# RWKV mixer: the key projection as three reduced matmuls on split operands in place of one fp32 matmul, and two buffers for gates and decays

## The chip, the cores and the metric

The kernel runs on one core of one Trainium2 chip. The metric is device microseconds of one execution; lower is better. Before the change three runs took 1544.76 to 1545.33 us, median 1544.91 us.

## The reference, cut to what matters

The program is one inference step of a two-layer decoder. Layer 0 mixes tokens with Mamba-2, layer 1 with RWKV-7; both are wrapped in SwiGLU blocks and end in a gated embedding. A prompt of 256 tokens and 8 samples of 4 tokens go through together as 288 columns, in float32. The part that the change touches is this:

```python
xx = u_prev - u
mixed = u[None] + xx[None] * mu[:, None, None, :]
xr, xw, xk, xv, xa, xg = mixed[0], mixed[1], mixed[2], mixed[3], mixed[4], mixed[5]
r = xr @ w_r
k = xk @ w_k
v = xv @ w_v
...
g = jax.nn.sigmoid(xg @ g1) @ g2
kk = heads(k * k_k)
decay = jnp.exp(-jnp.exp(heads(w)))
```

The weights r_wr, r_wk, r_wv are 1024 x 1024. The columns of k of one pair of heads feed the recurrence of that pair alone.

## The kernel before, in words

Activations lie features by tokens: 8 tiles of 128 features x 288 tokens. A product of weights and activations is made in one of two ways. `mm3` takes a weight tile that was split into a high part (`whi`, ScalarE, line 55) and a low part (`wlo`, VectorE, line 56), four tiles to a split, and an activation that was split likewise by `hilo` (lines 155 and 156), and issues three matmuls in the reduced type float32r (lines 147 to 149). A whole product takes the raw float32 weight from a second stream (`next_whole`) and the raw activation, and is one matmul instruction in float32, which the trace shows as two records. The split stream `ws` holds 224 tiles of the RWKV stage, the whole stream `wn` 88: 8 for `r_wa1`, 16 for `r_g1`, and 64 for `r_wk`. `ws.next` splits 16 tiles ahead of use.

The RWKV stage (lines 1046 and following) starts with `lead`, which makes `u` and `xx`, the token-shift difference, and the inputs of the decay and rate branches. Then, for each pair of heads p = 0 to 7, four generators are stepped in turn: `bulk` (decay, rate, and the projections k and r of pair p + 1), `bulk2` (gate and projection v of pair p), `prep` (the triangular solve's operands of pair p, with `scan`, `AA`, `BK`), and `chain` (the recurrence of pair p - 1, over four chunks, with small matmuls of 64 x 64). At p = 0, `mix` (line 1105) makes the mixed activations once for all pairs: for r and v it writes into a temporary `t` with two buffers that `hilo` then splits, for k it writes a float32 tile that is used as it is. `gates` (p = 0 alone) makes eight tiles `mg` and multiplies each by two whole tiles of `r_g1` (line 1082).

The framework's scheduler sets the order of each engine's instructions from these generators, so an edit at one place moves instructions everywhere in the stage. Each engine runs its own list in order. Three PSUM banks, 0, 1 and 7, serve the big products of the loop in turn.

The names in what follows: `lnb` holds constants of the sigmoid and comes from the constants that GpSimd makes out of a loaded table `r_const`; `sw` and `sa` are the decay's and rate's sigmoids; `rs_y` is the running sum of `sw` (line 1229); `E1` its exponential; `SVm`, `SAV` and `S` belong to `chain`.

Of the kernel before, what the change touches and what calls it, by code (L numbers as in the profile page):

```python
# [6 lines left out]
F32 = mybir.dt.float32  # L7
F32R = mybir.dt.float32r
# [8 lines left out]
KD = 8  # L17
KF = 22
# [969 lines left out]
def s84(ap):  # L988
    return ap.rearrange("p (b t) -> p b t", b=8)


class Rwkv:
# [81 lines left out]
    def gates(self):  # L1074

        nc, k = self.nc, self.k
        pg = [k.bank(n)[:, :NT] for n in "YR"]
        for kt in range(KD):
            m = [None] * kt + [self.t("mg", bufs=2)]
            self.mix(5, kt, m)  # L1080
            for i in range(2):
                nc.tensor.matmul(pg[i], k.wn.next_whole("r_g1", kt, i), m[kt], start=kt == 0, stop=kt == KD - 1)  # L1082
            yield
        t, u = k.tmp("s"), k.tmp("u")
        self.sigmoid(t, pg[0], 0.0)
        self.sigmoid(u[0:32], pg[1][0:32], 0.0)
        k.hilo(self.lgh, self.lgl, t)
        self.stack(self.lg2, u, slice(0, 32), slice(32, 64))
        yield
# [11 lines left out]
    def mix(self, i, kt, out):  # L1101

        k = self.k
        m = k.tmp("t") if out[kt] is None else out[kt]
        self.nc.vector.scalar_tensor_tensor(m, self.xx[kt], k.g(f"mu{i}")[:, kt:kt + 1], self.u[kt], ALU.mult, ALU.add)
        if out[kt] is None:
            if i == 0:
                out[kt] = k.A[8 + kt], k.A[16 + kt]
            else:
                if kt == 0:  # L1110
                    k.renew(24, 32)
                k.renew(32 + kt, 33 + kt)
                out[kt] = k.A[24 + kt], k.A[32 + kt]
            k.hilo(*out[kt], m)
# [9 lines left out]
    def proj(self, n, i, x, p):  # L1124

        k, d = self.k, self.d[p]
        ps = k.bank("main")[:, :NT]
        for kt in range(KD):
            if p == 0:
                self.mix(i, kt, x)  # L1130
            if n == "k":
                self.nc.tensor.matmul(ps, k.wn.next_whole("r_wk", kt, p), x[kt], start=kt == 0, stop=kt == KD - 1)  # L1132
            else:
                k.mm3(ps, k.ws.next("r_w" + n, kt, p), x[kt], kt == 0, kt == KD - 1)
            if kt < KD - 1:
                yield
        d[n] = self.t(n, bufs=2)
        k.act(d[n], ps, AF.Copy)
        yield

    def bulk(self, p):

        nc, k = self.nc, self.k
        col = slice(p, p + 1)
        if p == 0:
            k.renew(0, 8, F32)
            k.renew(8, 16)
            self.xk = k.A[0:8]
            self.xv, self.xr = [[None] * KD for _ in range(2)]
        d = self.d[p] = {}  # L1150
        for n, x, b in (("sw", self.lw, "w0"), ("sa", self.la, "a0")):
            ps = k.bank("main")[:, :NT]
            self.stacked(ps, k.ws.next("r_" + n[1] + "2", 0, p), x)
            d[n] = self.t(n)
            self.sigmoid(d[n], ps, k.g(b)[:, col])
        yield
        yield from self.proj("k", 2, self.xk, p)
        yield from self.proj("r", 0, self.xr, p)

    def bulk2(self, p):  # L1160

        nc, k = self.nc, self.k
        d = self.d[p]
        ps = k.bank("main")[:, :NT]
        k.mm3(ps, k.ws.next("r_g2a", 0, p), (self.lgh, self.lgl), True, False)
        self.stacked(ps, k.ws.next("r_g2b", 0, p), self.lg2, False)
        d["g"] = self.t("g", bufs=3)
        k.act(d["g"], ps, AF.Copy)
        yield
        yield from self.proj("v", 3, self.xv, p)  # L1170
        V, v = self.V, d["v"]
        SAV = d["SAV"] = self.t("SAV", [P, 2, 5, 64], bufs=2)
        k.act(s84(V)[:, :, 0:4], s84(v[:, 256:288]), AF.Copy)
        pv = k.bank("A")
        for ch in range(5):
            for h in range(2):
                rows = slice(64 * h, 64 * h + 64)
                nc.tensor.matmul(pv[rows, 64 * ch:64 * ch + 64], v[rows, 64 * ch:64 * ch + 64] if ch < 4 else V[rows],
                                 self.I[rows], start=True, stop=True)
        for h in range(2):  # L1180
            rows = slice(64 * h, 64 * h + 64)
            k.act(SAV[rows, h], pv[rows, :320].rearrange("p (c t) -> p c t", c=5), AF.Copy)
        yield
# [29 lines left out]
    def prep(self, p):  # L1213

        nc, k = self.nc, self.k
        d = self.d[p]
# [10 lines left out]

        c = k.tmp("rs_y")
        nc.vector.tensor_tensor_scan(c, self.scan, d["sw"], 0.0, ALU.mult, ALU.add)
        E1 = d["E1"] = self.t("E1", bufs=3)  # L1230
        E2, Ex = k.tmp("ss"), k.tmp("t")
        k.act(E1, c, AF.Exp, scale=-KAPPA)
        k.act(E2, c, AF.Exp, scale=KAPPA)
# [13 lines left out]
        nc.vector.scalar_tensor_tensor(rk, d["r"], k.g("r_k")[:, col], k2, ALU.mult, ALU.mult)  # L1247
        self.pad_mul(AR[:, :, 1], d["r"], E1, AR[:, 4, 0])
        nc.vector.tensor_tensor(kk, kk, y, ALU.mult)
# [15 lines left out]
        ps = [k.bank("A"), k.bank("A")]  # L1265
# [7 lines left out]
        ps = [k.bank("A"), k.bank("A")]  # L1273
# [17 lines left out]
        def chunks(i):  # L1291

            return 5 if i < 2 else 4
# [16 lines left out]
        def at(t):  # L1310
            return lambda ch: t[:, ch]
# [4 lines left out]
        ps = mms(at(XT), eye)  # L1316
        k.act(X, ps, AF.Copy)
        yield
        for i in range(1, 6):
            n = chunks(i)  # L1320
# [21 lines left out]
        ps = mms(full, eye)  # L1342
# [5 lines left out]
        ps = k.bank("A")[:, :320].rearrange("p (c t) -> p c t", c=5)  # L1348
# [7 lines left out]
        ps = mms(at(R), full)  # L1356
# [5 lines left out]
    def chain(self, p):  # L1362
# [3 lines left out]
        col = slice(p, p + 1)  # L1366
        AR, AA, BKt, SAV, TT, E1, S0 = self.AR[p % 2], d["AA"], d["BKt"], d["SAV"], d["TT"], d["E1"], d["S0"]
        H = [(h, slice(64 * h, 64 * h + 64), slice(64 - 64 * h, 128 - 64 * h)) for h in range(2)]
# [37 lines left out]
        def solved(ch):  # L1406
# [5 lines left out]
            if ch < 4 and S is not None:  # L1412
                st["Se"] = self.t("Se", [P, 64])
                k.act(st["Se"], S, AF.Copy, scale=E1[:, 64 * ch + 63:64 * ch + 64])

        def state(ch):

            ps, S = k.bank("R"), st["S"]
            e = E1[:, 64 * ch + 63:64 * ch + 64]
            for h, rows, _ in H:  # L1420
# [21 lines left out]
        def samples():  # L1442
# [8 lines left out]
            nc.vector.tensor_tensor(S0, S0, ps.rearrange("p (b i) -> p b i", b=8), ALU.add)  # L1451
            nc.vector.tensor_tensor(S0, S0, s84(E1[:, 256:288])[:, :, 3:4].to_broadcast([P, 8, 64]), ALU.mult)
            nc.sync.dma_start(k.io["wkv_s"][p], S0)
# [165 lines left out]
    return np.ascontiguousarray(v.reshape(-1, P).T)  # L1619


COUNT = {"ffn": 24 * KF, "ple": 80, "mamba": 520, "rwkv": 224}
WHOLE = {"rwkv": 88}


def weight_tiles(x, stages):
# [97 lines left out]
def launch(x, stages, run):  # L1724
# [5 lines left out]
          for n, a in ins.items()}  # L1730
    units = [-(-max(1, sum(c.get(s, 0) for s, _, _ in stages)) // UT) for c in (COUNT, WHOLE)]
    for n, u in zip(("w", "wn"), units):
# [21 lines left out]
```

## Time and profile before

| | |
|---|---|
| profiled execution | 1545.45 us, its span 1543.6 us |
| three runs | median 1544.91 us (1544.76 to 1545.33) |
| PE busy | 1524.0 us, 99% of the span |
| VectorE busy | 1099.9 us, 71% |
| ScalarE busy | 972.9 us, 63% |
| RWKV stage | from about 976 to about 1290 us of the span |

A matmul's record is longer than the time from its start to the next matmul's, since matmuls are pipelined; the chain of work that ended last cuts the records to what each adds, and its steps are used for PE here. The same holds to a lesser degree on VectorE and ScalarE, where the distance between starts is used.

### The profile page before, as it was taken

To read this page: it belongs to the slowest core of one execution; us is meant where nothing else is said; L and a number is where in the kernel's file an instruction comes from. 1 tells how busy PE (TensorE), PEld (TensorE's weight loads), DVE (VectorE), ACT (ScalarE), POOL (GpSimd) and SP (SyncE) were. 2 spreads that over 40 slices of the span, in tenths; PEclk is the share of its full clock that TensorE was granted. 3 is DMA by queue.
4 is the path that set the end of the run, shared out by engine and by line. 5 is a ranking of instruction groups with operands and counts; after the bars stand their busy time and mean duration, and the time that the engine had idled before them with its cause. 6 is when DMAs were issued, how large, how long until landed. Compare 5 with 4: busy or idle time off the path is not lost.

```text
span 1543.6 us, 35587 instructions
## 1 busy us (share of the span) xinstructions
PE 1524.0 (99%) x14178; PEld 1422.4 (92%) x14178; DVE 1099.9 (71%) x2321; ACT 972.9 (63%) x2217; POOL 46.0 (3%) x143
## 2 busy tenths in 40 slices
PE   9999999999999999999999999999999999999997
PEld 8999998989989999999999999777777778999997
DVE  7666578888888766656876655887766778666566
ACT  7555458989887655554755554766666746555545
POOL 0000003112100000000000000100000000000000
PEclk9999999999999999999999999999999999999999
DMA  7555563765665555555555555531222224555551
GB/s 245 168 169 166 164 213 116 248 221 198 228 223 197 171 166 165 166 168 171 161 170 168 168 164 164 178 109 59 78 84 65 63 72 153 170 168 165 164 168 57
DMA packets 75574, 243.48 MB, mean 158 GB/s; under 512 B 11728, under 2 KB 16976, under 8 KB 75408
## 3 DMA queue, kind: packets, MB, share of 16 engines
q1 hardware_dynamic: 75408, 241.21, 48.6%
q8 instruction: 111, 1.82, 0.5%
q14 instruction: 55, 0.45, 0.1%
HBM read 226.54 MB, written 14.64 MB: 156 GB/s over the span
## 4 chain that ended last, share of the span: by engine, by line
PE 93%; DVE 4%; DMA 1%; ACT 1%; issue 1%; SPq 0%; POOL 0%; DVEq 0%; POOLq 0%; ACTq 0%
PE bank L147 26%; PE bank L149 26%; PE bank L148 25%; PE bank L1307 2%; PE bank L1132 1%; PE bank L770 1%; PE bank L1449 1%; PE bank L1421 1%; PE bank L774 1%; PE bank L766 1%; PE bank L641 1%; PE bank L1187 1%; DVE wlo L56 1%; PE bank L1381 1%; PE bank L1082 0%
## 5 line engine op out<-in xcount | busy, mean ns | idle before, releaser
L147 PE MATMUL bank<-act,whi 128*128 128x288 f32 x2760 | 825.0, 300 | 6.2 <-ACT act L138 3.7
L148 PE MATMUL bank<-act,whi 128*128 128x288 f32 x2760 | 819.0, 297 | 1.3 <-DVE act L156 1.3
L149 PE MATMUL bank<-act,wlo 128*128 128x288 f32 x2760 | 814.9, 296 | 0.1
L55 ACT ACTIVATE whi<-raw 128x512 fp32r<-128x512 f32 x754 | 472.1, 631 | 434.6 <-PE bank L148 421.9
L56 DVE TENSOR_TENSOR wlo<-raw,whi 128x512 fp32r<-128x512 f32 x754 | 515.2, 689 | 263.5 <-ACT whi L55 236.6
L147 PEld LDWEIGHTS bank<-act,whi 128*128 128x128 f32 x2760 | 517.2, 188 | 15.1 <-ACT act L138 5.2
L148 PEld LDWEIGHTS bank<-act,whi 128*128 128x128 f32 x2760 | 521.6, 189 | 6.4 <-DVE act L156 2.1
L149 PEld LDWEIGHTS bank<-act,wlo 128*128 128x128 f32 x2760 | 520.9, 189 | 3.0 <-DVE wlo L56 0.3
L147 PE MATMUL bank<-more,whi 128*128 128x288 f32 x192 | 56.7, 295 | 0.0
L148 PE MATMUL bank<-more,whi 128*128 128x288 f32 x192 | 56.4, 294 | 0.0
L149 PE MATMUL bank<-more,wlo 128*128 128x288 f32 x192 | 56.4, 294 | 0.0
L321 DVE TENSOR_TENSOR t<-bank,rstd 128x288 f32<-128x288 f32 x88 | 39.8, 456 | 23.0 <-PE bank L149 23.0
L324 DVE TENSOR_TENSOR u<-bank,s 128x288 f32<-128x288 f32 x88 | 39.8, 456 | 22.7 <-PE bank L149 22.6
L671 DVE SCALAR_TENSOR_TENSOR conv_a<-X,vec,conv_a 128x312 f32<-128x312 f32 x96 | 50.9, 534 | 2.6 <-ACT conv_a L138 2.2
L138 ACT ACTIVATE s<-t 128x288 f32<-128x288 f32 x104 | 45.8, 443 | 6.2 <-DVE t L366 3.5
L138 ACT ACTIVATE X<-bank 128x256 f32<-128x256 f32 (+2 forms) x98 | 30.5, 338 | 21.8 <-PE bank L1307 20.8
L138 ACT ACTIVATE act<-h,vec 128x288 fp32r<-128x288 f32 (+1 forms) x71 | 37.1, 528 | 7.3 <-DMA h<-in_xT 2.7
L1132 PE MATMUL bank<-act,raw 128*128 128x288 f32 x128 | 40.8, 434 | 0.0
L148 PEld LDWEIGHTS bank<-more,whi 128*128 128x128 f32 x192 | 36.3, 189 | 0.0
L149 PEld LDWEIGHTS bank<-more,wlo 128*128 128x128 f32 x192 | 36.2, 189 | 0.0
L147 PEld LDWEIGHTS bank<-more,whi 128*128 128x128 f32 x192 | 36.0, 187 | 0.0
L1323 DVE TENSOR_TENSOR Z<-bank,lv 128x256 f16<-128x256 f32 (+1 forms) x40 | 17.5, 437 | 24.1 <-PE bank L1307 23.5
(383 smaller groups left out, 1736.8 us busy)
## 6 DMA issues: line engine op xcount, KB each, us to landing
raw<-in_w SPq DMA_DIRECT2D x377, 512.0 KB, 3.6
h0a<-in_ssm_a SPq DMA_DIRECT2D x16, 512.0 KB, 5.4
h0b<-in_ssm_b SPq DMA_DIRECT2D x16, 512.0 KB, 5.1
out_ssm_s<-h0b SPq DMA_DIRECT2D x16, 512.0 KB, 3.9
raw<-in_wn SPq DMA_DIRECT2D x11, 512.0 KB, 3.6
S<-in_wkv_in SPq DMA_DIRECT2D x8, 256.0 KB, 3.7
out_wkv_s<-S SPq DMA_DIRECT2D x8, 256.0 KB, 2.0
h<-in_xT SPq DMA_DIRECT2D x8, 144.0 KB, 4.6
```

The costliest lines, as they stand in the source:

```text
L55: nc.scalar.activation(hi, src, AF.Copy)
L56: nc.vector.tensor_tensor(lo, src, hi.bitcast(F32), ALU.subtract)
L138: i = self.nc.scalar.activation(out, in_, func, **kw)
L147: nc.tensor.matmul(ps, wh, xh, start=start, stop=False)
L148: nc.tensor.matmul(ps, wh, xl, start=False, stop=False)
L149: nc.tensor.matmul(ps, wl, xh, start=False, stop=stop)
L321: nc.vector.tensor_tensor(t, pg, r, ALU.mult)
L324: nc.vector.tensor_tensor(u, pu, s, ALU.mult)
L671: nc.vector.scalar_tensor_tensor(a[:, :312], X[:, t:t + 312], k.g(f"conv_w{t}")[:, ct:ct + 1], a[:, :312], ALU.mult, ALU.add)
L1132: self.nc.tensor.matmul(ps, k.wn.next_whole("r_wk", kt, p), x[kt], start=kt == 0, stop=kt == KD - 1)
L1307: nc.tensor.matmul(ps[rows, ch], lhs(ch)[rows], rhs(ch)[rows], start=True, stop=True)
L1323: nc.vector.tensor_tensor(Z[:, :n], pz, lv(i, n), ALU.mult)
```

## The change

r_wk moves from the whole stream to the split stream (224 to 288 split tiles, 88 to 24 whole ones). The activation xk is now made through the temporary `t` and split into `k.A[kt]` and a new tile `xkl`, and the k projection is issued as three float32r matmuls for each tile. Three tiles lose a buffer: `mg` has one in place of two, `g` two in place of three, `E1` two in place of three.

```diff
--- before.py
+++ after.py
@@ -1076,7 +1076,7 @@
         nc, k = self.nc, self.k
         pg = [k.bank(n)[:, :NT] for n in "YR"]
         for kt in range(KD):
-            m = [None] * kt + [self.t("mg", bufs=2)]
+            m = [None] * kt + [self.t("mg", bufs=1)]
             self.mix(5, kt, m)
             for i in range(2):
                 nc.tensor.matmul(pg[i], k.wn.next_whole("r_g1", kt, i), m[kt], start=kt == 0, stop=kt == KD - 1)
@@ -1106,6 +1106,8 @@
         if out[kt] is None:
             if i == 0:
                 out[kt] = k.A[8 + kt], k.A[16 + kt]
+            elif i == 2:
+                out[kt] = k.A[kt], self.t(f"xkl{kt}", dt=F32R)
             else:
                 if kt == 0:
                     k.renew(24, 32)
@@ -1128,10 +1130,7 @@
         for kt in range(KD):
             if p == 0:
                 self.mix(i, kt, x)
-            if n == "k":
-                self.nc.tensor.matmul(ps, k.wn.next_whole("r_wk", kt, p), x[kt], start=kt == 0, stop=kt == KD - 1)
-            else:
-                k.mm3(ps, k.ws.next("r_w" + n, kt, p), x[kt], kt == 0, kt == KD - 1)
+            k.mm3(ps, k.ws.next("r_w" + n, kt, p), x[kt], kt == 0, kt == KD - 1)
             if kt < KD - 1:
                 yield
         d[n] = self.t(n, bufs=2)
@@ -1143,10 +1142,8 @@
         nc, k = self.nc, self.k
         col = slice(p, p + 1)
         if p == 0:
-            k.renew(0, 8, F32)
-            k.renew(8, 16)
-            self.xk = k.A[0:8]
-            self.xv, self.xr = [[None] * KD for _ in range(2)]
+            k.renew(0, 16)
+            self.xk, self.xv, self.xr = [[None] * KD for _ in range(3)]
         d = self.d[p] = {}
         for n, x, b in (("sw", self.lw, "w0"), ("sa", self.la, "a0")):
             ps = k.bank("main")[:, :NT]
@@ -1164,7 +1161,7 @@
         ps = k.bank("main")[:, :NT]
         k.mm3(ps, k.ws.next("r_g2a", 0, p), (self.lgh, self.lgl), True, False)
         self.stacked(ps, k.ws.next("r_g2b", 0, p), self.lg2, False)
-        d["g"] = self.t("g", bufs=3)
+        d["g"] = self.t("g", bufs=2)
         k.act(d["g"], ps, AF.Copy)
         yield
         yield from self.proj("v", 3, self.xv, p)
@@ -1227,7 +1224,7 @@
 
         c = k.tmp("rs_y")
         nc.vector.tensor_tensor_scan(c, self.scan, d["sw"], 0.0, ALU.mult, ALU.add)
-        E1 = d["E1"] = self.t("E1", bufs=3)
+        E1 = d["E1"] = self.t("E1", bufs=2)
         E2, Ex = k.tmp("ss"), k.tmp("t")
         k.act(E1, c, AF.Exp, scale=-KAPPA)
         k.act(E2, c, AF.Exp, scale=KAPPA)
@@ -1619,8 +1616,8 @@
     return np.ascontiguousarray(v.reshape(-1, P).T)
 
 
-COUNT = {"ffn": 24 * KF, "ple": 80, "mamba": 520, "rwkv": 224}
-WHOLE = {"rwkv": 88}
+COUNT = {"ffn": 24 * KF, "ple": 80, "mamba": 520, "rwkv": 288}
+WHOLE = {"rwkv": 24}
 
 
 def weight_tiles(x, stages):
```

What the scheduler makes of it differs over the whole stage. VectorE at the start of the stage, up to the running sum `rs_y` of pair 0; before:

```order
L1105 SCALAR_TENSOR_TENSOR t_13656<-act_1206_13442,vec_129,act_1214_13450 128x288
L1119 TENSOR_SCALAR sw_13616<-bank_1269_13613,vec_129 128x288
L1119 TENSOR_SCALAR sa_13629<-bank_1271_13622,vec_129 128x288
L156 TENSOR_TENSOR act_1198_13434<-t_13656,act_1261_13605 128x288
L1105 SCALAR_TENSOR_TENSOR t_13663<-act_1207_13443,vec_129,act_1215_13451 128x288
L1105 SCALAR_TENSOR_TENSOR t_13670<-act_1208_13444,vec_129,act_1216_13452 128x288
L56 TENSOR_TENSOR wlo_13682<-raw_13238,whi_13681 128x512
L56 TENSOR_TENSOR wlo_13716<-raw_13272,whi_13715 128x512
L156 TENSOR_TENSOR act_1199_13435<-t_13663,act_1262_13606 128x288
L1229 SCALAR_TENSOR_TENSOR rs_y_13745<-scan_13576,sw_13616 128x288
```

and now:

```order
L1094 TENSOR_TENSOR la_13459<-s_13503,la_13459 64x288
L1094 TENSOR_TENSOR lw_13458<-s_13503,lw_13458 64x288
L56 TENSOR_TENSOR wlo_13738<-raw_13272,whi_13737 128x512
L1121 TENSOR_SCALAR sw_13616<-bank_1269_13613,vec_129 128x288
L1121 TENSOR_SCALAR sa_13629<-bank_1271_13622,vec_129 128x288
L156 TENSOR_TENSOR xkl_1277_13645<-t_13643,act_1254_13598 128x288
L1105 SCALAR_TENSOR_TENSOR t_13651<-act_1208_13444,vec_129,act_1216_13452 128x288
L1105 SCALAR_TENSOR_TENSOR t_13659<-act_1209_13445,vec_129,act_1217_13453 128x288
L1105 SCALAR_TENSOR_TENSOR mg_13812<-act_1206_13442,vec_129,act_1214_13450 128x288
L1226 SCALAR_TENSOR_TENSOR rs_y_13801<-scan_13576,sw_13616 128x288
```

Before, the eight mixes of k stand ahead of these rows and r is being split here. Now the second tile of k is split here (`xkl`), the third and fourth are only mixed, and the first `mg` has come ahead of `rs_y`.

ScalarE at the same place, behind the copy of `lw`; before:

```order
L138 ACTIVATE lw_13458<-s_13503 64x288
L133 ACT_TABLE_LOAD
L138 ACTIVATE act_1261_13605<-t_13656 128x288
L138 ACTIVATE sw_13616<-sw_13616 128x288
L138 ACTIVATE k_13653<-bank_1273_13634 128x288
L138 ACTIVATE sw_13616<-sw_13616,lnb_13582 128x288
L138 ACTIVATE sa_13629<-sa_13629 128x288
L138 ACTIVATE sw_13616<-sw_13616 128x288
L138 ACTIVATE sa_13629<-sa_13629,lnb_13582 128x288
L138 ACTIVATE act_1262_13606<-t_13663 128x288
L138 ACTIVATE sa_13629<-sa_13629 128x288
```

and now:

```order
L138 ACTIVATE lw_13458<-s_13503 64x288
L133 ACT_TABLE_LOAD
L138 ACTIVATE act_1254_13598<-t_13643 128x288
L138 ACTIVATE sw_13616<-sw_13616 128x288
L138 ACTIVATE sw_13616<-sw_13616,lnb_13582 128x288
L138 ACTIVATE sa_13629<-sa_13629 128x288
L138 ACTIVATE sw_13616<-sw_13616 128x288
L138 ACTIVATE sa_13629<-sa_13629,lnb_13582 128x288
L138 ACTIVATE act_1255_13599<-t_13651 128x288
L138 ACTIVATE sa_13629<-sa_13629 128x288
L138 ACTIVATE act_1256_13600<-t_13659 128x288
```

The three copies `act<-t` are high parts: of r before, of the second, third and fourth tile of k now. The third of k stands behind the four steps of `sw` and `sa` that begin with the one that reads `lnb`.

PE in the recurrence of the fourth pair, where the small 64 x 64 matmuls of the chain's second chunk begin; before:

```order
L1395 MATMUL bank_1786_16280<-S_16243,AR_1250_13590 64x64 x2
L1397 MATMUL bank_1786_16280<-SAV_15782,AA_15595 64x64 x2
L1401 MATMUL bank_1757_16124<-AR_1250_13590,S_16243 64x64
L1263 MATMUL bank_1780_16208<-AR_1249_13589,BK_13591 64x128
L1263 MATMUL bank_1781_16209<-AR_1249_13589,BK_13591 64x128
L1401 MATMUL bank_1757_16124<-AR_1250_13590,S_16243 64x64
L1393 MATMUL bank_1788_16289<-r_const_13561,q_16141 64x64 x2
L1397 MATMUL bank_1788_16289<-SAV_15782,AA_15595 64x64 x2
L1132 MATMUL bank_1825_16481<-act_1253_13597,raw_15259 128x288
L1132 MATMUL bank_1825_16481<-act_1254_13598,raw_15259 128x288
```

and at the same place of the following pair in the changed kernel, where the lines of the small ones are three lower:

```order
L148 MATMUL bank_1751_16153<-act_1199_13435,whi_15741 128x288
L1392 MATMUL bank_1685_15791<-S_15754,AR_1249_13589 64x64 x2
L1394 MATMUL bank_1685_15791<-SAV_15269,AA_15082 64x64 x2
L1260 MATMUL bank_1679_15721<-AR_1250_13590,BK_13591 64x128
L1260 MATMUL bank_1680_15722<-AR_1250_13590,BK_13591 64x128
L1398 MATMUL bank_1656_15635<-AR_1249_13589,S_15754 64x64 x2
L1390 MATMUL bank_1687_15800<-r_const_13561,q_15652 64x64 x2
L1394 MATMUL bank_1687_15800<-SAV_15269,AA_15082 64x64 x2
L149 MATMUL bank_1751_16153<-act_1262_13606,wlo_15742 128x288
L147 MATMUL bank_1751_16153<-act_1263_13607,whi_15829 128x288
L148 MATMUL bank_1751_16153<-act_1200_13436,whi_15829 128x288
L1406 MATMUL bank_1693_15836<-rhs_15798,TT_15608 64x64 x2
```

Before, whole k products (line 1132) stand behind the block of small matmuls. Now it is r products that stand there, and the three matmuls of one tile are parted by the small ones.

## Rows read from the trace of the kernel before

**Rows 1.** The page's busy times over the whole span (us, share, instructions).
```profile
PE 1524.0 (99%) x14178; PEld 1422.4 (92%) x14178; DVE 1099.9 (71%) x2321; ACT 972.9 (63%) x2217; POOL 46.0 (3%) x143
```

**Rows 2.** Windows: length, PE, PEld, DVE, ACT, POOL busy (instructions), PE clock, DMA, GB/s.
```profile
978.00:1011.00 33.00, 29.01 (x148) 20.92 (x147) 32.33 (x87) 24.04 (x76) 6.33 (x18) 0.95 0.45 147
992.00:996.00 4.00, 1.89 (x7) 0.79 (x6) 3.95 (x9) 3.86 (x11) 3.53 (x13) 1.00 0.45 149
996.00:1000.00 4.00, 3.65 (x12) 2.71 (x13) 4.00 (x10) 3.71 (x10) 0.00 (x0) 0.65 0.34 125
1098.60:1132.30 33.70, 33.09 (x511) 24.33 (x510) 23.41 (x67) 21.67 (x59) 0.00 (x0) 1.00 0.21 66
1132.30:1164.00 31.70, 31.40 (x479) 23.41 (x475) 23.72 (x66) 21.68 (x60) 0.00 (x0) 1.00 0.28 86
```

**Rows 3.** Chain that ended last, from 1068 to 1086 us: start, us, what.
```profile
1068.16 0.27 PE bank L1307 x10
...
1070.03 0.33 PE bank L147
1070.36 0.13 PE bank L148
1070.49 0.13 PE bank L149
...
1075.46 0.28 DVE S L1424
...
1076.17 0.43 DVE sw L1119
...
1078.09 1.20 DVE wlo L56 x2
...
1080.92 0.66 DVE rs_y L1229
...
1081.60 0.68 DVE SVm L1439
...
1083.12 0.27 PE bank L1395 x2
...
1083.57 1.17 PE bank L1132 x4
1084.74 0.26 PE bank L1409 x4
1085.00 0.68 PE bank L1132 x2
```

**Rows 4.** VectorE in order of time, three stretches of the stage's start.
```profile
986.79 1.37 DVE L1105 SCALAR_TENSOR_TENSOR act<-act,vec,act 128x288 f32<-128x288 f32 x3
988.08 0.44 DVE L1069 TENSOR_TENSOR s<-s,bank 128x288 f32<-128x288 f32 x1
...
1000.39 0.82 DVE L156 TENSOR_TENSOR act<-t,act 128x288 fp32r<-128x288 f32 x2
1001.13 0.51 DVE L1105 SCALAR_TENSOR_TENSOR t<-act,vec,act 128x288 f32<-128x288 f32 x1
```

**Rows 5.** Chain that ended last, from 985 to 1016 us.
```profile
985.74 5.31 DMA r_const<-in_r_const
...
993.19 0.04 POOL lnb L1036
993.23 0.52 ACT sw L138
993.75 0.33 ACT sa L138
994.09 0.33 ACT sw L138
...
995.83 0.67 DVE rs_y L1229
...
998.41 1.10 PE bank L1082 x2
...
1003.39 0.48 PE bank L1082 x2
...
1010.23 0.61 DVE AA L1269
1010.84 0.14 issue
1010.97 1.42 PE bank L1263 x44
1012.40 2.80 PE bank L1082 x10
```

**Rows 6.** ScalarE and VectorE in order of time, the buffer of g.
```profile
1069.66 0.40 ACT L138 ACTIVATE g<-bank 128x288 f32<-128x288 f32 x1
...
1070.48 0.45 DVE L1488 TENSOR_TENSOR act<-rstd,g 128x288 f32<-128x288 f32 x1
```

## The prediction

> **What bounds the kernel now.** I read the page's busy times first, then the windows over the RWKV stage, then the chain of work that ended last in it, then VectorE and ScalarE in order of time where the chain leaves PE. Outside the stage nothing is edited, so only the stage counts.
>
> PE is busy 99% of the span [rows 1], but that figure counts overlapping records. The windows part the stage in two. At its start, from 978 to 1011 us, VectorE is busy 32.33 of 33 us and PE has gaps: in one stretch of 4 us it works 1.89 [rows 2]. This head is **VectorE's**: it makes all mixed activations here. In the loop over pairs, one pair takes 31.7 to 33.7 us, VectorE is busy 23.4 to 23.7 of it, ScalarE 21.7, PE nearly all [rows 2]. The chain of one pair shows PE throughout, except for one section of 7.66 us, from 1075.46 to 1083.12, that runs through VectorE from `S` by way of `wlo`, `rs_y` and `SVm` [rows 3]. So a pair is **PE's** with one VectorE section. A change of 3.1 us (0.2%) is about what a measurement of this kernel can tell from none.
>
> **Prices.** A float32r matmul adds 0.13 us to the chain, 0.33 when it is the first behind small 64 x 64 ones [rows 3]; mm3 is 3 x 0.132 = 0.396 us. The whole product's two records: four take 1.17, two 0.68 [rows 3], so a pair is 0.49 and 0.19 is paid on entering; I take 0.488. The change saves 0.092 us of PE for each tile. Entering big matmuls costs 0.33 - 0.13 = 0.20; entering small ones about 0.11 (ten take 0.27 behind a big one [rows 3], at 0.016 each once running): 0.155 for a switch on average, bounds 0.11 and 0.20. On VectorE a mix costs 0.43 (three from 986.79 to 988.08), a low part 0.37 (two from 1000.39 to 1001.13) [rows 4], a `wlo` 0.60 [rows 3].
>
> **The head.** Up to the first `AA` the order of instructions gives VectorE eight `xkl` and three `wlo` more, and two `mg` fewer, which come behind: 8 x 0.37 + 3 x 0.60 - 2 x 0.43 = 3.9 us. VectorE idles 0.67 us in this window, so 3.2 to 3.9 reaches the first `AA` at 1010.23 [rows 5], from which the chain is PE's again; I take 3.9, since those idles are semaphore gaps. ScalarE gets eight copies of 0.34 and three `whi`; it has 9 us free in the window [rows 2], so their number costs nothing, but their place does. `lnb` arrives at 993.19 behind the load of `r_const` (5.31 us) and GpSimd's constants [rows 5], which the change doesn't touch. ScalarE's new order puts the third high part of k behind the step that reads `lnb`, and VectorE puts `rs_y` behind only two mixes and an `mg` after `xkl`. Adding up VectorE's new rows from 985.7 us, it comes to `rs_y` at about 993.6; `sw` is ready at 994.09 + 0.33 = 994.4, so it waits some 0.9 us (bounds 0 and 1.3) where it had mixes to do before. Behind `AA`, PE has three more gate matmuls to do and one mm3 of v fewer, 3 x 0.488 - 0.396 = +1.1, against the eight tiles of pair 1, -0.7: +0.3 (bounds -0.7 and +1.1). Pair 0's k products lie in PE's gaps either way. Head: 3.9 + 0.9 + 0.3 = **+5.1**.
>
> **The loop.** Six pairs remain: 48 x 0.092 = **-4.4** on PE. But the new order parts the big matmuls more often: counted from the first `chain` to the last small matmul, it switches between big and small 318 times where the old does 292. 26 x 0.155 = **+4.0** (2.9 to 5.2). In the VectorE section the rows from `S` to the last `AA` grow: mostly two `wlo` where there were one or two, and both `SVm` where there was one, while `sw` leaves. Priced row by row over five pairs that is +2.8 us; PE does r products under it, as it did k products, and where PE ends the section it costs nothing. Between 0 and 2.8 I take the middle, **+1.4**. Outside the section the 16 added splits lie beside PE, with VectorE 9 us free a pair; that cover is gone only if `wlo` comes late, and then the next mm3 waits.
>
> **Buffers.** `g` is written at 1069.66 and the last reader of the buffer before the last starts at 1070.48 [rows 6], so with two buffers the copy comes some 1.3 us later; the PSUM bank behind it is one of three and the next-but-one product starts several us on: 0 (at worst 0.8 a pair). `E1` waits for the older pair's last multiply; only `prep`'s later rows read it: 0. `mg` with one buffer makes each mix wait for two gate matmuls; the order has put other rows between: 0 here, and a rival below. The loads are the same number and the queue is half empty: 0.
>
> **Sum.** 5.1 - 4.4 + 4.0 + 1.4 = +6.1 us on the profiled execution's 1545.45, so 1551.5; that execution is 0.5 above the median, so **1551.0 us**. With all lower bounds +1.0 (3.2 + 0 - 0.7 - 4.4 + 2.9), with all upper +9.9 (3.9 + 1.3 + 1.1 - 4.4 + 5.2 + 2.8): 1546 to 1555.
>
> **Rivals.** (a) *PE's total decides, faster.* VectorE's lost head is made up later, because PE is given its backlog in a pair in which it has gaps, and the added switches fall into waits that PE had anyway. Then 64 x 0.092 = 5.9 us go: 1539.0. For it: PE is on the chain almost everywhere. Against: the head is VectorE's at 98% [rows 2], and PE behind it has no known gap of 5 us. It decides if PE's idle behind 1012 us is over 5 us. The Trainium skill (FP8 and Floating Point Precision, section TensorE Precision Notes) counts four passes for true FP32; by that a whole product would be 4 x 0.132 = 0.528, the saving 0.132 a tile, and the loop's first term -6.3, the sum +4.2. The rows, with 0.488, show less. (b) *Half made up, no change to be told.* The section of VectorE costs 0 and the switches 2.9, the head 3: 3 - 4.4 + 2.9 = +1.5, or 1546.4. (c) *The clock and the single `mg`, slower still.* PE works little ahead of 996 us and then runs for 4 us at a granted 0.65 on average, between its levels of 1.2 and 2.4 GHz [rows 2]; a gate matmul takes 1.10 there and 0.48 later [rows 5]. Now k trickles in at VectorE's pace, so PE idles sooner and the low stretch may last some 4 us longer: 2 to 4 us, and with one `mg`, VectorE's list stands behind the gate matmuls for up to 0.5 each, 2 us over the rest of them. About +10.5: 1555.5.
>
> **How the numbers follow.** Forecast 0.50, (a) 0.13, (b) 0.22, (c) 0.15. Slower by over 0.2% means above 1548.0: the forecast nearly whole, and (c). Faster 0.12, same 0.23, slower 0.65. The range takes in the forecast's bounds, (b), and (c): 1544.5 to 1557.0.
>
> **What would show it.** In the new profile: VectorE near 98% busy from 978 to about 1016, the first `AA` at about 1015, and an idle of VectorE ahead of `rs_y` with ScalarE named; pairs of about 32.5 us on average, no shorter; line 1132's records gone. I am wrong if the first `AA` comes before 1013, if pairs shorten by 0.7 or more, or if PE waits on `wlo` in the loop.

## The result and the profile after

The changed kernel takes 1557.98 us, the median of four runs (1555.34 to 1561.47), where the kernel before takes 1544.84 in four runs beside it (1544.12 to 1545.33). The ratio is 1.0087, with a 95% interval of 1.0066 to 1.0107: 13.1 us slower. The forecast was +6.1 us, 1551.0; the sign was right, the size about half, and the time lies one microsecond outside the range. The profiled execution took 1558.19 us, its span 1556.3. Two executions far from all others, 2409 us of h2 and 5147 us of f2, are left out of the medians further down.

The page's busy times of the changed kernel answer to [rows 1]:

```profile
PE 1531.6 (98%) x14242; PEld 1434.9 (92%) x14242; DVE 1112.9 (72%) x2345; ACT 984.3 (63%) x2241; POOL 45.4 (3%) x143
```

VectorE has 24 instructions and 13 us more, as the edit says. PE is busy 7.6 us longer, although float32r products are cheaper than whole ones; this figure counts overlapping records, so it is not PE's work.

**Where the 12.7 us of span went.** Four marks cut the program: the start of the RWKV stage (VectorE's first multiply that makes `u`), the first and the last 128 x 512 `AA`, and the first matmul of the block behind the stage. The table has the starts in the profiled executions of six kernels; e1, g1, h1 and f1 are described in the next section.

| us | before | after | e1 | g1 | h1 | f1 |
|---|---|---|---|---|---|---|
| start of the stage | 978.65 | 980.67 | 980.81 | 980.41 | 982.24 | 979.47 |
| to the first `AA` | 31.50 | 37.48 | 31.69 | 37.31 | 37.35 | 36.77 |
| to the last `AA` | 234.26 | 238.12 | 236.20 | 237.01 | 238.50 | 234.15 |
| to the next block's first matmul | 47.67 | 46.22 | 52.13 | 46.26 | 46.97 | 47.03 |
| to the end | 251.52 | 253.81 | 251.47 | 251.51 | 253.74 | 253.98 |
| span | 1543.6 | 1556.3 | 1552.3 | 1552.5 | 1558.8 | 1551.4 |

Nothing ahead of the stage was edited, and its start wanders by 3.6 us between kernels that are the same up to there, so the first row's 2.0 us belong to the execution: from 100 to 300 us the granted clock was 1.00 in before and f1, and 0.98 or 0.99 in the four that start later. The rest is the head with +6.0, the loop with +3.9, the tail with -1.4, and +2.3 behind the tail, where nothing was edited either.

**The head.** Windows from the start of the stage to the first `AA`, columns as in [rows 2]; the kernel before:

```profile
978.65:1010.15 31.50, 27.96 (x141) 20.21 (x139) 30.90 (x84) 23.39 (x74) 6.33 (x18) 0.95 0.44 143
```

and the changed kernel, with two stretches inside it:

```profile
980.67:1018.15 37.48, 30.98 (x142) 21.91 (x140) 35.03 (x92) 27.45 (x84) 4.58 (x18) 0.82 0.38 125
...
1008.00:1012.00 4.00, 2.63 (x10) 1.62 (x11) 3.98 (x13) 2.83 (x7) 0.00 (x0) 0.83 0.00 0
1012.00:1016.00 4.00, 4.00 (x12) 2.52 (x13) 2.50 (x9) 0.44 (x1) 0.00 (x0) 0.50 0.00 0
```

VectorE's busy time grows by 35.03 - 30.90 = 4.1 us, and its idle time from 0.60 to 2.45. Where it idles is shown by VectorE in order of time in the changed kernel:

```profile
994.99 0.76 DVE L1105 SCALAR_TENSOR_TENSOR mg<-act,vec,act 128x288 f32<-128x288 f32 x1
995.67 0.74 DVE L1226 TENSOR_TENSOR_SCAN rs_y<-scan,sw 128x288 f32<-128x288 f32 x1
...
1012.69 0.45 DVE L1248 TENSOR_TENSOR rs_q<-rs_q,sa 128x288 f32<-128x288 f32 x1
...
1014.64 0.52 DVE L1105 SCALAR_TENSOR_TENSOR mg<-act,vec,act 128x288 f32<-128x288 f32 x1 [1.50 <-PE bank L1082]
1018.15 1.29 DVE L1266 TENSOR_TENSOR AA<-bank,r_const 128x512 f32<-128x512 f32 x2 [0.73 <-PE bank L1260]
```

and PE at that place:

```profile
1012.48 2.12 PE L1082 MATMUL bank<-mg,raw 128*128 128x288 f32 x4
```

There is no idle ahead of `rs_y`: the scan starts right behind the `mg`, and `sw` had been ready just before, as ScalarE's row shows:

```profile
995.11 0.43 ACT L138 ACTIVATE sw<-sw 128x288 f32<-128x288 f32 x1
```

The idle comes later. At 1014.64 a mix has waited 1.50 us for the only `mg` buffer, because the gate matmuls that read the one before run in 1012 to 1016 at a granted 0.50, the 1.2 GHz level; four records take 2.12 us. VectorE's list, `AA` at its end, stands behind it.

**The loop.** One pair from `AA` to `AA`, two of them, answers to the last lines of [rows 2]:

```profile
1088.50:1123.00 34.50, 34.11 (x514) 26.66 (x512) 25.85 (x69) 24.09 (x66) 0.00 (x0) 1.00 0.26 79
1123.00:1156.50 33.50, 33.22 (x505) 25.54 (x503) 24.80 (x69) 22.43 (x63) 0.00 (x0) 1.00 0.27 81
```

PE is as full as before, and VectorE and ScalarE have one to two microseconds more to do in a pair. A piece of the chain of work that ended last, in the changed kernel:

```profile
1096.71 0.20 PE bank L1392 x2
1097.09 0.33 PE bank L148
1097.41 0.27 PE bank L1304 x10
1097.69 0.33 PE bank L149
1098.15 0.26 PE bank L1406 x4
1098.41 0.33 PE bank L148
1098.87 0.29 PE bank L1304 x10
1099.19 0.44 ACT X L138
1099.62 0.33 ACT XT L138
```

Single float32r matmuls stand between small ones, and each costs 0.33 us there, not 0.13: the switches that the prediction counted. Counted in PE's rows from the first `AA` to the next block, big and small matmuls take turns 398 times where they did 373 times before, 25 more. What that costs in time no run below parts from the rest.

**The tail.** PE in order of time at the end of the stage, in the changed kernel:

```profile
1294.64 0.33 PE L1418 MATMUL bank<-SAV,BKt 128*64 128x64 f32 x2 [0.33 <-DVE SAV L1407]
...
1295.89 0.40 PE L1184 MATMUL bank<-ch,center 128*128 128x288 f32 x1 [0.56 <-ACT ch L138]
...
1302.49 0.85 PE L147 MATMUL bank<-act,whi 128*128 128x288 f32 x2 [3.67 <-ACT act L138]
```

and in the kernel before:

```profile
1292.08 1.06 PE L147 MATMUL bank<-act,whi 128*128 128x288 f32 x6 [1.34 <-ACT act L138]
```

Both start the next block 46 to 48 us behind the last `AA`. The whole stretch, in the kernel before and in the changed one:

```profile
1244.41:1292.08 47.67, 46.16 (x597) 36.24 (x597) 32.69 (x83) 23.63 (x61) 0.00 (x0) 0.96 0.25 80
...
1256.27:1302.49 46.22, 39.85 (x547) 29.21 (x543) 30.55 (x79) 21.50 (x57) 0.00 (x0) 0.94 0.26 82
```

PE has 6.3 us less to do here and the stretch is only 1.4 us shorter, so PE's work does not set most of its length; the latency of the last pair does. The 50 matmuls that are gone are big ones of the output products, 16 to 17 tiles of three: they now stand ahead of the last `AA`, in the loop. At 0.13 us each they are some 6.5 us of PE, so the loop's +3.9 and the tail's -1.4 belong together, +2.5. Before, output products filled PE until shortly ahead of the next block. Now they have run out by 1294, PE idles longer, and the next block begins at a low clock. Two windows of the changed kernel:

```profile
1296.00:1304.00 8.00, 3.42 (x10) 2.35 (x11) 3.42 (x9) 2.72 (x6) 0.00 (x0) 0.58 0.32 96
1302.00:1308.00 6.00, 5.51 (x24) 5.51 (x25) 4.45 (x11) 3.34 (x8) 0.00 (x0) 0.53 0.66 197
```

The chain there, in the changed kernel, shows what a low clock does to a matmul's step, 0.24 in place of 0.13:

```profile
1301.99 0.45 ACT act L138
1302.49 0.85 PE bank L147 x2
1303.34 0.25 PE bank L148
1303.59 0.24 PE bank L149
...
1307.83 0.13 PE bank L147
```

Some twenty matmuls at 0.11 us too much are 2.2 us, and the table's last stretch grows by 2.3.

### The profile page after: what moved, and what is told of

Read it like the earlier page. It is cut to its first block, busy times and chain, and to the rows that moved or that the text cites. A ratio compares the mean times of both kernels' runs of the same rounds, so it can differ in the third digit from the quotient of the medians.

```text
span 1556.3 us, 35779 instructions
## 1 busy us (share of the span) xinstructions
PE 1531.6 (98%) x14242; PEld 1434.9 (92%) x14242; DVE 1112.9 (72%) x2345; ACT 984.3 (63%) x2241; POOL 45.4 (3%) x143
## 4 chain that ended last, share of the span: by engine, by line
PE 94%; DVE 3%; ACT 1%; DMA 1%; issue 1%; SPq 0%; DVEq 0%; ACTq 0%
PE bank L147 26%; PE bank L149 26%; PE bank L148 26%; PE bank L1304 2%; PE bank L1260 1%; PE bank L770 1%; PE bank L1446 1%; PE bank L1418 1%; PE bank L1082 1%; PE bank L774 1%; PE bank L766 1%; PE bank L641 1%; PE bank L1406 1%; PE bank L1184 1%; DVE wlo L56 1%
## 5 line engine op out<-in xcount | busy, mean ns | idle before, releaser
L147 PE MATMUL bank<-act,whi 128*128 128x288 f32 x2824 | 848.2, 301 | 7.6 <-ACT act L138 6.0
L149 PE MATMUL bank<-act,wlo 128*128 128x288 f32 x2824 | 837.4, 297 | 0.1
L148 PE MATMUL bank<-act,whi 128*128 128x288 f32 x2760 | 819.5, 297 | 1.1 <-DVE act L156 1.0
L55 ACT ACTIVATE whi<-raw 128x512 fp32r<-128x512 f32 x770 | 482.1, 631 | 435.0 <-PE bank L148 419.5
L56 DVE TENSOR_TENSOR wlo<-raw,whi 128x512 fp32r<-128x512 f32 x770 | 526.2, 689 | 261.3 <-ACT whi L55 234.4
L147 PEld LDWEIGHTS bank<-act,whi 128*128 128x128 f32 x2824 | 531.0, 188 | 18.2 <-ACT act L138 8.3
L149 PEld LDWEIGHTS bank<-act,wlo 128*128 128x128 f32 x2824 | 534.7, 189 | 4.0 <-DVE wlo L56 0.3
L148 PEld LDWEIGHTS bank<-act,whi 128*128 128x128 f32 x2760 | 522.6, 189 | 6.4 <-DVE act L156 2.4
L159 DVE SCALAR_TENSOR_TENSOR act<-h,vec,act 128x288 fp32r<-128x288 f32 x56 | 28.3, 512 | 6.4 <-ACT act L138 6.3
```

Source lines behind the costliest of these rows:

```text
L55: nc.scalar.activation(hi, src, AF.Copy)
L56: nc.vector.tensor_tensor(lo, src, hi.bitcast(F32), ALU.subtract)
L147: nc.tensor.matmul(ps, wh, xh, start=start, stop=False)
L148: nc.tensor.matmul(ps, wh, xl, start=False, stop=False)
L149: nc.tensor.matmul(ps, wl, xh, start=False, stop=stop)
L159: nc.vector.scalar_tensor_tensor(lo, src, scale, hi.bitcast(F32), ALU.mult, ALU.subtract)
```

## The experiments

Eleven kernels ran, and the table has all of them. Ratios are to the kernel before on the same chip, with the 95% interval.

| kernel | median us | ratio |
|---|---|---|
| after | 1557.98 | 1.0087 (1.0066 to 1.0107) |
| e1: before, with the three buffer cuts | 1548.14 | 1.0021 (1.0010 to 1.0032) |
| g1: e1, with pair 0's k split | 1553.33 | 1.0051 (1.0033 to 1.0069) |
| e2: after, `EARLY` 1 | 1555.74 | 1.0063 (1.0048 to 1.0078) |
| e3: after, all buffers back, a split buffer fewer | 1561.75 | 1.0107 (1.0090 to 1.0124) |
| e4: after, pair 0's k whole, its split later | 1566.93 | 1.0134 (1.0117 to 1.0152) |
| f1: after, two `mg` | 1554.14 | 1.0068 (1.0042 to 1.0094) |
| f2: after, three `E1` | 1555.88 | 1.0071 (1.0053 to 1.0089) |
| f3: after, `RATE` 1.2 | 1565.25 | 1.0127 (1.0103 to 1.0151) |
| h1: after, k with two matmuls a tile | 1560.13 | 1.0106 (1.0090 to 1.0121) |
| h2: after, k with one whole matmul a tile | 1555.77 | 1.0071 (1.0054 to 1.0088) |
| h3: f1 with `RATE` 1.7 | 1559.12 | 1.0088 (1.0071 to 1.0105) |

**The buffers alone, in the kernel before.**

```diff
-            m = [None] * kt + [self.t("mg", bufs=2)]
+            m = [None] * kt + [self.t("mg", bufs=1)]
...
-        d["g"] = self.t("g", bufs=3)
+        d["g"] = self.t("g", bufs=2)
...
-        E1 = d["E1"] = self.t("E1", bufs=3)
+        E1 = d["E1"] = self.t("E1", bufs=2)
```

> The kernel before with the three smaller buffer counts alone (mg 1, g 2, E1 2); k stays a whole fp32 product. Theory H (VectorE's longer head lets the fill of PE run ahead of the chain, so that the last chain is left without cover and the clock falls): buffers are nothing, 1543 to 1546 us. Theory B (E1 with two buffers holds prep back behind the older pair, and this is what sets the chain late): most of the 13 us is here, 1552 to 1558, with PE idle of 5 us or more behind the last r_wo product.

Measured: 1548.14 us in ten runs against 1544.85, ratio 1.0021 with an interval clear of 1; it lies between the two ranges that were expected. So the buffers cost about 3.3 us where the prediction had 0. Its profiled execution took 1554.23, six above the median. PE ran at a low clock for 16 us behind the last `AA` at 1248.70, and that stretch is 52.13 us long where it was 47.67:

```profile
1256.00:1264.00 8.00, 8.00 (x147) 5.59 (x147) 4.16 (x11) 4.02 (x13) 0.00 (x0) 1.00 0.33 105
1264.00:1272.00 8.00, 8.00 (x85) 6.12 (x82) 4.04 (x11) 3.65 (x10) 0.00 (x0) 0.56 0.01 2
1272.00:1280.00 8.00, 8.00 (x72) 6.88 (x72) 3.86 (x9) 2.30 (x5) 0.00 (x0) 0.58 0.21 66
```

The loop ahead of it is undisturbed, with a clock of 1.00 from the first to the last `AA`:

```profile
1012.50:1248.70 236.20, 232.89 (x3436) 173.34 (x3436) 174.98 (x472) 156.44 (x428) 0.00 (x0) 1.00 0.25 78
```

It takes 236.20 us against 234.26 before, and the head 31.69 against 31.50. So in this one execution some 1.9 us of the buffers' price lie in the loop and next to nothing in the head.

**Pair 0's split alone**, on top of e1: pairs 1 to 7 keep the whole product of k on the float32 tile.

```diff
-            if p == 0:
+            if n == "k" and p == 0:
+                k0 = k.A[24 + kt], self.t(f"xkl{kt}", dt=F32R)
+                self.mix(i, kt, x)
+                k.hilo(*k0, x[kt])
+                k.mm3(ps, k.ws.next("r_wk", kt, p), k0, kt == 0, kt == KD - 1)
+            elif p == 0:
                 self.mix(i, kt, x)
```

> The kernel before with the smaller buffer counts, and only pair 0's k product as three reduced matmuls on split xk and split weights; pairs 1 to 7 keep whole fp32 products. It parts head from loop. If the head's VectorE work is what matters: 3.9 us over the run with buffers alone, 1551 to 1554, first AA 4 to 6 us later. If the loop's split of k carries the loss: 1547 to 1550.

Measured: 1553.33 us, ratio 1.0051. Less e1's 1.0021 this leaves 0.30%, 4.6 us, for pair 0's split (1.4 to 7.9 with both intervals). The trace has the same head as the changed kernel, 37.31 us to the first `AA` against 37.48, although the idles of VectorE stand at other rows and the clock is another one: the head is as long as VectorE's list with its waits, whichever those are. Its tail is covered like that of the kernel before, and the time from there to the end is the 251.5 of before:

```profile
1300.99 1.06 PE L147 MATMUL bank<-act,whi 128*128 128x288 f32 x6 [1.33 <-ACT act L138]
```

What is left of the change's 1.0087 is 0.36%, 5.6 us (1.4 to 9.7), for splitting k in pairs 1 to 7. In the profiled executions the difference between g1 and after is 3.8 us of span: 2.3 behind the tail, 1.1 in the loop, the rest at start and head. The loop's 1.1 is no clean price. In g1 the pair from 1154.70 to 1190.21 took 35.51 us, where its neighbours took 33.26 and 32.84, and PE ran at a low clock inside it though it was busy throughout:

```profile
1168.00:1172.00 4.00, 4.00 (x68) 3.18 (x66) 3.04 (x8) 3.44 (x11) 0.00 (x0) 1.00 0.28 78
1172.00:1176.00 4.00, 4.00 (x61) 3.02 (x58) 2.68 (x9) 2.33 (x7) 0.00 (x0) 0.72 0.00 2
1176.00:1180.00 4.00, 4.00 (x31) 3.38 (x33) 1.65 (x4) 2.52 (x6) 0.00 (x0) 0.50 0.43 131
```

**The head over all kernels.** Ten kernels, the changed one among them, split k of pair 0; their profiled executions take 35.2 to 38.3 us from the stage's start to the first `AA`. The three that do not (before, e1, e4) take 31.0 to 31.7. So the split of pair 0 lengthens the head by some 3.5 to 7 us, although VectorE's waits in it stand at different rows in these kernels.

**Is PE the bound of the loop?** Two kernels change PE's work for k in pairs 1 to 7 in opposite directions and leave the splits on VectorE and ScalarE. In h1 the product with the low weight goes:

```diff
+            if n == "k" and p > 0:
+                wh, _ = k.ws.next("r_wk", kt, p)
+                self.nc.tensor.matmul(ps, wh, x[kt][0], start=kt == 0, stop=False)
+                self.nc.tensor.matmul(ps, wh, x[kt][1], start=False, stop=kt == KD - 1)
```

> The changed kernel with the product of the low weights left out of k in pairs 1 to 7 (56 matmuls of 0.13 us, 7.4 us of PE; all splits on ScalarE and VectorE stay). If PE's total decides the loop, 1550 to 1553. If the latency of prep and chain decides and k is only fill, PE merely idles more: 1556 to 1561, with the tail at least as bare.

and in h2 one float32 matmul on the high parts takes the place of the three:

```diff
+            if n == "k" and p > 0:
+                wh, _ = k.ws.next("r_wk", kt, p)
+                self.nc.tensor.matmul(ps, wh.bitcast(F32), x[kt][0].bitcast(F32), start=kt == 0, stop=kt == KD - 1)
```

> The changed kernel with k of pairs 1 to 7 as one fp32 matmul on the high parts alone (the two low products are left out; the splits, their loads and the buffers stay), so PE has the whole product's 0.49 in place of 0.40 for each of 56 tiles, 5.2 us more, and fewer switches. If PE's total decides the loop, 1561 to 1564. If k is fill under the chain's latency, 1554 to 1559, and against pair 0 alone split (1553.3) it prices the added splits in the loop.

By the prices of [rows 3] h1 has 56 x 0.132 = 7.4 us less of PE, h2 56 x 0.092 = 5.2 more. The scheduler orders each of these kernels anew: big and small matmuls take turns 374 times in h1 and 372 in h2, against 398 in the changed kernel, so h2's balance is smaller if switches cost what the prediction gave them. Measured on one chip: h1 1560.13, h2 1555.77. The kernel with less PE work is, if anything, the slower one, and neither differs from the changed kernel beyond its interval. Both times lie in the ranges that were given to k as fill, but the windows are less clear. Those from the second to the sixth `AA`, four pairs, and from there to the last, two pairs, show what became of the work. First the changed kernel:

```profile
1055.96:1188.87 132.91, 132.05 (x2021) 102.85 (x2021) 101.24 (x273) 91.96 (x249) 0.00 (x0) 1.00 0.27 82
1188.87:1256.27 67.40, 67.31 (x1022) 52.71 (x1024) 52.88 (x144) 44.99 (x122) 0.00 (x0) 1.00 0.25 81
```

h1, with two windows inside the second stretch:

```profile
1055.49:1190.84 135.35, 133.71 (x2037) 104.67 (x2034) 105.59 (x281) 96.68 (x264) 0.00 (x0) 1.00 0.28 89
1190.84:1258.09 67.25, 61.55 (x955) 46.94 (x954) 49.71 (x139) 39.81 (x111) 0.00 (x0) 0.90 0.22 65
...
1236.00:1246.00 10.00, 7.79 (x162) 5.81 (x159) 6.91 (x20) 7.51 (x23) 0.00 (x0) 0.80 0.17 49
1246.00:1256.00 10.00, 10.00 (x102) 8.51 (x98) 6.45 (x22) 3.65 (x9) 0.00 (x0) 0.69 0.01 2
```

h2 from the second to the last `AA`, and from there to the next block:

```profile
1051.40:1250.88 199.48, 197.99 (x2959) 146.17 (x2960) 152.83 (x411) 135.81 (x370) 0.00 (x0) 0.99 0.24 77
1250.88:1301.93 51.05, 48.20 (x590) 37.40 (x586) 33.08 (x84) 22.98 (x60) 0.00 (x0) 0.93 0.24 75
```

In h1's first four pairs PE is as full as in the changed kernel. It has not less to do there but later work earlier: 343 big float32r matmuls (of k, r, v, the gate and the output) stand in them against 333. So these four pairs say nothing on whether PE sets their length. What is missing shows in the last two: 117 such matmuls against 184, 5.7 us of idle against 0.1, and the same length, 67.25 against 67.40. There less PE work did not make a pair shorter. But the clock was low from 1236 to 1256, which by the two windows takes 10 x 0.20 + 10 x 0.31 = 5.1 us of PE's time at full clock, an estimate; without it these pairs might have been shorter. h2 does not show that its added work fits in for free. At its last `AA` it has 140 of the big matmuls still to do where the changed kernel has 97, and its tail is 51.05 us long, also with a stretch of low clock.

What h1 shows, then, is that 7.4 us less of PE bought no time as measured, because it turned into idle and low clock in the last pairs. That k is fill in every pair, whose pace costs nothing, is not shown, and g1's pair at a low clock, two to three microseconds longer than its neighbours, speaks against it.

**The tail and the rate of the fill.** `EARLY` is the number of output tiles begun before the last pair, `RATE` the number of fill steps for each round of `prep` and `chain`. e2 changes `EARLY = 3` to 1, f3 `RATE = 1.45` to 1.2, h3 takes f1 (below) and sets `RATE` to 1.7.

> The changed kernel with EARLY 1 in place of 3: two output tiles of r_wo (12 tile products of 0.4 us, 4.8 us of PE) stay for the last iteration instead of the one before. Theory H and B alike hold that the tail lacks fill: PE's idle behind the last product falls from 8 to about 3 us and the low clock after it goes, while the pair before gets shorter by what was taken from it if PE is its bound: 1550 to 1554. If the tail's idle does not cost (rival: the chain's start alone sets the end), the time stays at 1555 to 1560.

> The changed kernel with RATE 1.2 in place of 1.45: fewer fill steps of PE for each step of prep and chain, the rest at the pair's end. Theory H (the fill runs ahead of the chain and is missing at the end): the last chain starts earlier against the fill, PE's idle in the tail shrinks from 8 us to under 5: 1549 to 1555. Rival (the generators' steps matter little to the scheduler, or the pair's own latency then shows): 1556 to 1562.

> The changed kernel with two mg buffers and RATE 1.7 in place of 1.45. RATE 1.2 cost 7 us, so the fill of a pair is needed early (the next prep waits for k and r). If that goes on beyond 1.45, 1549 to 1553; if 1.45 is the turning point, 1554 to 1559.

Measured: e2 1555.74, 2.2 less than the change with overlapping intervals, and its wait of PE ahead of the next block is 2.90 us in place of 3.67. f3 1565.25, 7 us slower and above both ranges that were expected: its second `AA` comes 84.1 us behind the stage's start, against 75.3 in the change and 69.4 before. Fewer fill steps delay what the next pair's `prep` needs, the other way from what a cure would need. h3 1559.12 against 1554.14 for f1. No setting tried cured the tail.

**The single `mg`, the `E1`, and all buffers.** f1 and f2 put back one buffer each; the room comes from temporaries that were 320 columns wide and use 288.

```diff
-        t = self.work.tile([P, 320], dt, tag=tag, name=self.nm(tag), bufs=n)
+        w = 320 if tag in ("t", "u") else NT
+        t = self.work.tile([P, w], dt, tag=tag, name=self.nm(tag), bufs=n)
...
-            m = [None] * kt + [self.t("mg", bufs=1)]
+            m = [None] * kt + [self.t("mg", bufs=2)]
```

> The changed kernel with two buffers for mg again, paid for by narrower scratch tiles (the same instructions in the same order but for what the buffer frees). In the changed trace VectorE waits 1.50 us at 1013 for a gate matmul that runs at half clock. If the single mg and the clock cost the head its 2 us beyond VectorE's work, the first AA comes 1.5 to 2.5 us sooner and the time falls to 1554 to 1557; if the head is VectorE's work alone, nothing beyond 1 us.

> The changed kernel with three buffers for E1 again, paid for likewise. The buffers alone cost the kernel before 3.3 us, most of it in the loop. If that is E1, the stretch from the second to the last AA falls from 200.3 to about 198 us and the time by 2 to 4, to 1553 to 1556; if it is g or mg, no change: 1556 to 1560.

Measured: f1 1554.14, ratio 1.0068; f2, which has three `E1` and one `mg`, 1555.88, ratio 1.0071. Both intervals overlap that of the change. In f1 the wait for `mg` is gone, and so is the low clock behind 1000 us. Yet its head is only 0.7 us shorter, 36.77 against 37.48. The window from 1000 to 1020 us, in f1:

```profile
1000.00:1020.00 20.00, 16.88 (x147) 12.25 (x146) 19.43 (x53) 10.86 (x27) 0.00 (x0) 1.00 0.08 27
```

and in the changed kernel:

```profile
1000.00:1020.00 20.00, 17.08 (x122) 11.61 (x124) 17.68 (x46) 9.35 (x24) 0.00 (x0) 0.82 0.08 26
```

The second `AA` comes 71.3 us behind the start of the stage, not 75.3. That is about the 3.8 us between the medians, but h3 has two `mg` as well and its second `AA` comes at 75.9, and f2 has one and comes at 73.0, so the buffer alone is not shown to give them back.

e3 puts all three buffers back and pays with one of the eight buffers of split weights (`wsp`, 8 to 7).

> The changed kernel with the three buffer counts of before (mg 2, g 3, E1 3), paid for by 7 in place of 8 buffers of split weights. Theory B: the loss goes nearly, 1544 to 1548. Theory H: 1555 to 1560, no change beyond noise, since the split of k at the head is still there.

Measured: 1561.75, slower than the change by the medians and above both expected ranges. It has the second `AA` early like f1, at 70.9 us, but takes 205.5 to the last one where the change takes 200.3. The loss of the eighth split buffer is mixed with the three that are back, so this run says nothing of them.

**Pair 0's k whole, and the splits behind the gate.** e4 gives pair 0 the raw tile and the whole weights; the eight splits for the later pairs follow the gate matmuls.

```diff
+            if n == "k" and p == 0:
+                self.mix(i, kt, self.xraw)
+                self.nc.tensor.matmul(ps, k.wn.next_whole("r_wk", kt, p), self.xraw[kt], start=kt == 0,
+                                      stop=kt == KD - 1)
...
                 yield from w.gates()
+                yield from w.ksplit()
```

> The changed kernel with pair 0 of k as whole fp32 products on the raw xk, and the eight splits of xk moved behind the gate matmuls, where VectorE has idle time. Theory H: the first AA comes near 1012 instead of 1018 us, the chain is no longer late against the fill, 1544 to 1549. Theory B: the head gains at most its 4 us, the tail stays bare, 1553 to 1557.

Measured: 1566.93, the slowest of all, ten microseconds above the higher range that was expected. The first `AA` is back at 31.0 us, so the splits are indeed what lengthens the head. But the second comes at 80.3 where the change has 75.3: in the new place the splits stand ahead of pair 0's v and pair 1's k in the fill, and pair 1's `prep` waits for those. Here the work that was moved from in front of one latency chain to in front of the next one cost more there.

None of these beats the kernel before, which stays the best version.

## Why the prediction was right in sign and wrong in size

**The head: right.** Forecast +5.1, of it 4.8 to the first `AA`. The trace has 6.0 to the first `AA`, g1 less e1 has 4.6 for the split of pair 0 alone, and over all kernels it is some 3.5 to 7. Its main term, 3.9 us of VectorE's rows, came out at 4.1, with just the instructions that were counted. The second term failed: "it waits some 0.9 us" ahead of `rs_y` did not happen. `rs_y` came 15.0 us behind the stage's start, as summed, but `sw` was ready 14.9 us behind it, not 15.8 as in the sum. VectorE waited elsewhere, 1.50 us for `mg` and 0.73 for PE's `AA` products, so that the head came out near the forecast is in part luck. Those waits are the mechanism of rival (c), the low clock and the single `mg`; its place and its half-speed gate matmuls are in the trace, and its time, 1555.5, came nearest of all cases. Its prices are not confirmed: g1 has the same head without that wait for `mg`, and two `mg` in f1 shorten the head by 0.7 us alone.

**The loop: +1.0 forecast, "So a pair is PE's" unsettled.** Loop and tail together grew by 2.5 us, with the buffers' share in it. The 26 more switches are there (25 by the traces' rows), and each matmul is as cheap as priced, but whether a pair is PE's remains open, and with it whether "-4.4 on PE" and the switches' +4.0 reach the time. The windows showed PE nearly all busy, and the chain ran along PE; a chain that is followed back through a full engine lists all its work alike, needed at once or not. h1 took 7.4 us out and gained nothing, which is against the -4.4 as a gain of time; g1's pair at a low clock is for PE. That the loop's sum came out near is therefore luck as far as these runs go. The prediction also treated the loop and what follows it as apart, while the scheduler moved some 50 output matmuls from the tail into the loop.

**The step that failed: buffers at 0.** This is the largest term missing from the sum, and e1, which has nothing but the three buffer cuts, shows it: about 3.3 us (1.5 to 4.9 by its interval). The argument looked at the copy into `g` and took `E1` as read late and `mg` as covered. Which of the three costs it in the kernel before was not separated. In the changed kernel the two that were put back, `mg` and `E1`, gave 3.8 and 2.1 us by the medians, both inside the noise.

**The second missing term: behind the stage.** "Outside the stage nothing is edited, so only the stage counts" is true of the edit but not of the clock. The changed kernel, f1 and h1, with waits of 3.67 or 3.68 us ahead of the next block, take 253.7 to 254.0 us from its first matmul to the end; before and g1, with 1.34 and 1.33, take 251.5. h1's rows are:

```profile
1305.06 0.85 PE L147 MATMUL bank<-act,whi 128*128 128x288 f32 x2 [3.68 <-ACT act L138]
```

and the window behind it:

```profile
1300.00:1310.00 10.00, 6.13 (x22) 5.49 (x23) 5.70 (x14) 5.16 (x12) 0.00 (x0) 0.50 0.51 153
```

The wait alone does not settle it: e1 waited 2.81 us and took 251.5, h2 waited 2.80 and took 253.1.

With +3.3 for the buffers and +2.3 for the stretch behind the tail, the forecast's +6.1 would have been +11.7 against 13.1 measured.

**The rivals.** (a), that PE's total decides, fell with the result, and h1, with 7.4 us less of PE, was no faster than the changed kernel. The Trainium skill (FP8 and Floating Point Precision, section TensorE Precision Notes) counts four passes for true FP32, by which the saving would have been larger than the rows' 0.092 a tile, 0.132 as an estimate. No run here can tell the two apart by the time; the rows' 0.488 us stays the measured price. (b), half made up, fell with the result.

**What would have shown it wrong.** The first `AA` came at 1018, not before 1013; the pairs lengthened, from 32.7 us to 33.4 on average, and did not shorten; PE did not wait on `wlo` in the loop. So none of the signs of being wrong appeared. Of the signs for it two failed: the idle ahead of `rs_y`, and VectorE at 98% in the head, where it was busy 35.03 of 37.48 us. The fault lay where no sign had been named: in the buffers and behind the stage.

**Open:** which of `g`, `E1` and `mg` costs the 3.3 us, whether PE's pace or latency sets a pair, and what lowers the clock in pairs in which PE is busy. The 2.8 us that g1's loop grows by fit the two disturbances named above, the buffers (1.9 in e1's loop) and the one pair at a low clock. That VectorE's additional one to two microseconds a pair cost time in the loop is not shown: h2 and g1 both have one whole product a tile in pairs 1 to 7 and differ mainly by the added splits, and their ratios, 1.0071 and 1.0051, are not apart beyond their intervals.

## What to carry to other kernels

Price each buffer that is taken away by a run of that cut alone, since an argument from one writer and one reader gave 0 here where the run showed 3.3 us. Before a saving on a busy engine is counted, ask whether its work there is needed at once or is fill under a latency chain. A kernel that leaves some of that work out is a first test, but where a scheduler orders everything anew, count what the engine did in the same stretch, and look at the clock, before its length is compared: in h1 four pairs were full again with work from later ones. Look behind the edited stage too: here fill ran out ahead of its end, and a block that nobody edited began at half speed and took 2.3 us longer.

## What was not expected of the hardware

PE's granted clock was 0.50, the 1.2 GHz level, from 1012 to 1016 us although PE had worked 2.63 of the 4 us before and worked all of these 4; a float32 gate product of two records then took 2.12 / 2 = 1.06 us where [rows 5] have 0.48. In e1's profiled execution the clock stood at 0.56 and 0.58 for 16 us behind the last `AA`, after eight microseconds in which PE was busy throughout, and in g1 it stood at 0.72 and 0.50 from 1172 to 1180, PE being busy before and in it. So a low clock did not only follow idle stretches in these runs, and what lowered it there is not known. Of waits of PE ahead of the next block, 1.33 and 1.34 us (g1, before) and 2.81 us (e1) left the rest of the program at 251.5 us, while 3.67 and 3.68 us in three kernels went with 2.2 to 2.5 us more.
